# Rope keys of the latent attention spread by transfers within SBUF, and block 2's selection rows written by ScalarE instead of GpSimd

## The chip, the cores and the metric

The kernel runs on one core of one Trainium2 chip. The metric is the device time of one execution in microseconds, as the median of several runs. A core has five engines that each work through their own instructions in order: TensorE (PE; its weight loads are listed apart as PEld), VectorE (DVE), ScalarE (ACT), GpSimd (POOL) and SyncE (SP, which here only issues transfers). ACT and POOL issue transfers too, from the same queue in which their arithmetic stands.

## The reference, cut to what matters

The input is 512 tokens of width 1024. Two layers of a first kind of block are followed by two layers of a second kind.

```
for l in range(2):      # first kind
    c_q, c_kv, k_r, ... = split(x @ w_in)        # latents of MLA; mLSTM; SSD
    q = rmsnorm(c_q) @ w_uq                      # 8 heads x (64 nope + 32 rope)
    k_nope, v = split(rmsnorm(c_kv) @ w_ukv)
    k_rope = rope(k_r)                           # ONE rope key, the same for all 8 heads
    s = (q_nope . k_nope + q_rope . k_rope) * 96 ** -0.5 ;  o = softmax(s) @ v
    x = layernorm(alpha * x + concat(o, mlstm, ssd) @ w_out)
    x = layernorm(alpha * x + moe(x))            # 16 experts in 4 groups, top 2
for l in range(2):      # second kind
    x = x + attention2(rmsnorm(x))               # several kinds of heads, two with differences
    x = x + swiglu(rmsnorm(x))                   # fg, fu, fd
```

The rope key of a token is shared by the eight heads of the latent attention (MLA). All of it is computed in float32, which the kernel reaches by splitting each operand into a high and a low f16 half and adding three matmuls.

## The kernel before, in words

Everything runs on chip memory (SBUF) in tiles of 128 partitions. A token block is 128 tokens, so there are four of them, called t0 to t3. Each projection loads a 128x1024 piece of the weights (`wst`), splits it on ACT (`wh`, L135) and DVE (`wl`, L136), and multiplies with three matmuls (L151 to L153) into PSUM. Normalisations take a reciprocal square root by an integer guess and Newton steps on DVE, a few small instructions that depend on each other (helper lines L159 to L170; the tiles end in `_rs` and `_rsq`). The program is written once, and a scheduler sets the order of the instructions on each engine from it when it is built. An instruction then starts when its engine has come to it and what it reads is there.

`mla()` runs in both layers of the first kind. It makes eight tiles `mlak`: for four heads a high and a low one. The lower 64 partitions get the head's own keys (`mlak<-gK`, L145 on ACT and L146 on DVE), and the upper 64 the shared rope keys `krh`, which POOL copies in once (L674), before any head's own keys are known. A head h uses tile h % 4, so the rope half serves both rounds. The first reader is the matmul `sM` (L703). Beside the start of this function the program still works on the SSD part: `xs` is normalised (L980, after the small steps on `ssd_rs`) and transposed by PE (`mixT`, L298), and POOL copies `mqz` (L1028) for the mLSTM.

`mix2()` runs in both layers of the second kind. It makes two tiles `kl` of 128x4x512 in f16, which carry on half of their partitions a head's low key halves and on the other half selection rows: a constant pattern `selq` that lets the matmul over `kl` (L1864) take the row maxima off the scores. At the start of each layer both tiles are filled with the pattern whole (L1556), and the key half is written later for each group of heads. What stands around it at layer 0: the end of the mixture of experts, whose sums `ysum` (L1438, L1440) go through a layernorm (`ln_...`, `mx`) and the rmsnorm (`xn_...`, `xn`, L236 on ACT, L242 on DVE) into the transposes `xT` (L184) and their eviction `xTh` (L145). At layer 1 the tiles are free earlier than the layer begins, so the scheduler puts the filling into the attention of layer 0 (its softmax: `pe` L761, `pt` L764 and L765, and `o` L800 and L804) and what follows is the projection of layer 0's mixed heads (`px`, loaded from `res` by a transfer that ACT issues, L321).

Of the kernel before, what the change touches and what calls it, by code (L numbers as in the profile page):

```python
# [12 lines left out]
F16 = mybir.dt.float16  # L13
BF16 = mybir.dt.bfloat16
I32 = mybir.dt.int32
AF = mybir.ActivationFunctionType
# [5 lines left out]
P = 128  # L22
T = 512
# [24 lines left out]
class Kern:  # L48
# [377 lines left out]
    def mixer1(self, l, cur):  # L426
# [12 lines left out]
        with self.pool("la") as la:  # L439
# [19 lines left out]
            with r("qm") as qm, r("m1") as m1:  # L459
                with r("s1") as self.q1, r("s2") as s2:  # L460
                    sd = self.ssd_tiles()
                    for b in (2, 4, 0, 3, 5, 1):
                        self.ssd_conv(b, pr, xh, xl, cC, cD, sd, u)
                    self.ssd_gate(xh, xl, cC, sd, u)
                    c0, c1 = (self.ssd_core(s2, m1, g, pr, sd, u) for g in range(2))
                    for c in (c0, c1, c0, c1, c0, c1, c0, c1):
                        next(c, None)
                cE = load("wB", 3, 512)
                cB = load("wB", 0, 512)
                ml = self.mlstm_proj(qm, pr, xh, xl, cE, cB, u)  # L470
                mo = [self.p2.tile([P, NT, P], F32, tag="mo", name="mo", bufs=2) for i in range(2)]
                og = ml[-1]
                with r("ml") as p:
                    self.ptp, self.npt = p, (5, 2)
                    mla = self.mla(p, l, lat)
                    next(mla)
                    for h in range(4):
                        self.mlstm_head(m1, h, mo[h // 2], *ml)
                        if h > 1:
                            (self.mlstm_norm(0, mo[0], og) if h == 2 else self.mix_part(p1, 4, mo[0]))  # L480
                        if h == 3:
                            self.mlstm_norm(1, mo[1], og)
                        next(mla, None)
                    self.mix_part(p1, 5, mo[1])
                    for _ in mla:
                        pass
# [179 lines left out]
    def mla(self, p1, l, lat):  # L666

        nc, p2 = self.nc, self.p2
        cq, ckv, krh = lat

        Kt = [[p1.tile([P, T], F16, name="mlak%d%d" % (h, i)) for i in range(2)] for h in range(4)]
        for h in range(4):
            for i in range(2):
                nc.gpsimd.tensor_copy(Kt[h][i][64:128], krh[i][64:128])  # L674
        wq = [self.wload(self.ap["w_uq"][l], 2048, WS_UQ) + (2,)]
        wkv = [self.wload(self.ap["w_ukv"][l], 1024, WS_UKV) + (1,)]
        v = self.values(p1, "mlav", 8, 64, 0, 8)
        for t in range(NT):
            ps = self.acc("gV")
            self.mm3(ps, ckv[0][:, 0, t * P:(t + 1) * P], ckv[1][:, 0, t * P:(t + 1) * P],  # L680
                     wkv[0][0][:, 512:1024], wkv[0][1][:, 512:1024], True, True)
            self.put_values(v, t, ps, 1.0 / (AS * WS_UKV))
        scale = 96.0 ** -0.5
        HG = 2
        Q, K = {}, {}

        def project(g):

            mx = self.max_tile()
            for i, h in enumerate(range(g * HG, (g + 1) * HG)):  # L690
                Q[h] = [p1.tile([P, T], F16, tag="mq%d" % i, name="mlaq%d" % i, bufs=4) for i in range(2)]
                K[h] = Kt[h % 4]
                ps = self.fm_gemm(cq[0], cq[1], wq, 1024, h * P, P, "gQ")
                tmp = p2.tile([P, T], F32, tag="tmp", name="qtmp", bufs=2)
                nc.vector.tensor_tensor(tmp, ps, self.tab, op=ALU.mult)
                self.split(Q[h][0], Q[h][1], tmp, 1.0 / WS_UQ)
                if h % 2 == 0:
                    kps = self.fm_gemm(ckv[0], ckv[1], wkv, 1024, h * 64, P, "gK")
                self.split(K[h][0][0:64], K[h][1][0:64], kps[64 * (h % 2):64 * (h % 2) + 64],
                           1.0 / WS_UKV)  # L700
                for t in range(NT):
                    ps = self.acc("sM")
                    nc.tensor.matmul(ps, Q[h][0][:, t * P:(t + 1) * P], K[h][0], start=True, stop=True)  # L703
                    nc.vector.tensor_reduce(mx[:, t, i:i + 1], ps, axis=AX.X, op=ALU.max)  # L704
            nc.vector.tensor_scalar(mx[:, :, :HG], mx[:, :, :HG], -1.0 / 256, None, op0=ALU.mult)
            mrow = p2.tile([P, T], F16, tag="mrow", name="mrow")
            nc.scalar.activation(mrow, self.max_rows(mx), AF.Copy)
            return mrow

        mrow = project(0)  # L710
        for g in range(8 // HG):
            yield
            nrow = project(g + 1) if (g + 1) * HG < 8 else None
            for i, h in enumerate(range(g * HG, (g + 1) * HG)):
                pt = self.softmax_T(
                    lambda s, ps, st: [
                        self.mm3(ps, K[h][0][:, s * P:(s + 1) * P], K[h][1][:, s * P:(s + 1) * P],
                                 Q[h][0], Q[h][1], True, False),
                        nc.tensor.matmul(ps, self.sel[:, i, :], mrow, start=False, stop=True)],
                    scale, [0] * NT, v[0] is None)  # L720
                o = self.pso("o")
                for t in range(NT):
                    self.pv(o[:, t * 66:t * 66 + 65], [(pt[s], t, self.value(v, s, h)) for s in range(NT)])
                if h % 2 == 0:
                    mx_ = p1.tile([P, NT, P], F32, tag="mo", name="mo")
                self.norm_out(o, 66, 64, mx_[:, :, 64 * (h % 2):64 * (h % 2) + 64])
                if h % 2:
                    self.mix_part(p1, h // 2, mx_)
            mrow = nrow
# [820 lines left out]
    def mix2(self, l, cur):  # L1550
        nc, b1 = self.nc, self.b1
# [1 line left out]
        u = 1.0 / (AS * WS_IN)  # L1553
        self.kl2, self.turn2 = [b1.tile([P, 4, T], F16, name="kl2%d" % i) for i in range(2)], 0
        for kl in self.kl2:
            nc.gpsimd.tensor_copy(kl, self.selq.unsqueeze(2).to_broadcast([P, 4, T]))  # L1556

        gq = b1.tile([P, 6, 64], F32, name="qkg")
        self.bcast_row(gq.rearrange("p a b -> p (a b)"), self.ap["qk_g"][l], 384)
# [501 lines left out]
```

## Time and profile before

| what | value |
|---|---|
| median of 3 runs (lowest, highest) | 2430.69 us (2425.39, 2432.09) |
| the profiled execution, its own time | 2429.33 us |
| span in its trace | 2427.6 us |
| mean granted clock of TensorE | 0.966 |
| instructions | 34940 |

All rows below come from that one profiled execution. Its span is 1.7 us shorter than its own time, and its own time is 1.4 us below the median of the runs. Times in the rows are counted from the start of the span.

### The profile page before, as it was taken

How to read it: one execution, taken by the hardware profiler on the slowest of the kernel's cores; microseconds unless marked ns; L12 is line 12 of the kernel's file. 1: busy time of each engine (PE TensorE's matmuls, PEld its weight loads, DVE VectorE, ACT ScalarE, POOL GpSimd, SP SyncE). 2: the span in 40 equal slices, each digit the busy share in tenths (PEclk: the TensorE clock that was granted, in tenths of full speed). 3: DMA queues.
4: the chain of work that ended last, by engine and by line, in shares of the span. 5: the costliest groups of instructions: out<-in, count | busy, mean ns of one | idle time of the engine just before them, and what ended most of it. 6: DMA issues, size and time to landing. Idle time of an engine off the chain costs nothing.

```text
span 2427.6 us, 34940 instructions
## 1 busy us (share of the span) xinstructions
PE 2218.0 (91%) x13462; PEld 1215.2 (50%) x13462; DVE 1690.5 (70%) x3602; ACT 1148.7 (47%) x1965; POOL 288.9 (12%) x345
## 2 busy tenths in 40 slices
PE   8888979888889789879998999999998989999999
PEld 4545546544546455434455554444444556544444
DVE  7978887778978977778999654442569996544421
ACT  5546648736547557725544433332345455422220
POOL 2221023231311133211000100000001000000000
PEclk9999989999999989989999999999999989999999
DMA  5311479943312769832212252222332112422222
GB/s 185 119 65 45 174 261 292 313 157 105 115 42 79 276 216 316 295 117 91 87 44 87 77 183 103 94 98 97 118 104 72 51 70 72 164 103 104 104 81 76
DMA packets 61278, 318.80 MB, mean 131 GB/s; under 512 B 12369, under 2 KB 12625, under 8 KB 32688
## 3 DMA queue, kind: packets, MB, share of 16 engines
q1 hardware_dynamic: 41600, 267.87, 31.0%
q0 software_dynamic: 14896, 31.85, 4.9%
q10 hardware_dynamic: 4608, 16.78, 1.8%
q8 instruction: 107, 1.75, 0.3%
q14 instruction: 67, 0.55, 0.1%
HBM read 290.78 MB, written 35.09 MB: 134 GB/s over the span
## 4 chain that ended last, share of the span: by engine, by line
PE 41%; DVE 10%; issue 5%; ACT 5%; DMA 3%; POOL 1%; POOLq 0%; ACTq 0%; DVEq 0%
PE fd L151 3%; PE fd L153 3%; PE fd L152 3%; PE fg L152 3%; PE fu L152 3%; PE fg L153 3%; PE fu L153 3%; PE fg L151 3%; PE fu L151 3%; PE o L800 2%; DMA res<-yt,sidx 2%; DVE wl L136 1%; PE gqk L151 1%; PE gqk L152 1%; PE gqk L153 1%
## 5 line engine op out<-in xcount | busy, mean ns | idle before, releaser
L136 DVE SCALAR_TENSOR_TENSOR wl<-wst,wh 128x1024 f16<-128x1024 f32 (+1 forms) x428 | 514.9, 1231 | 196.8 <-ACT wh L135 195.8
L135 ACT ACTIVATE wh<-wst 128x1024 f16<-128x1024 f32 (+1 forms) x428 | 429.7, 1047 | 270.8 <-PE fd L153 107.2
L152 PEld LDWEIGHTS <-wh 128*128 128x128 f16 x968 | 95.5, 99 | 102.2 <-issue 4.3
L153 PEld LDWEIGHTS <-wl 128*128 128x128 f16 x968 | 95.6, 99 | 101.4 <-issue 2.8
L151 PEld LDWEIGHTS <-wh 128*128 128x128 f16 x968 | 95.9, 99 | 99.8 <-issue 2.1
L152 PE MATMUL fd<-wl,fhh 128*128 128x512 f16 x352 | 133.6, 379 | 0.0
L153 PE MATMUL fd<-wh,fhl 128*128 128x512 f16 x352 | 133.6, 379 | 0.0
L151 PE MATMUL fd<-wh,fhh 128*128 128x512 f16 x352 | 133.6, 379 | 0.0
L151 PE MATMUL gqk<-wh,xTh 128*128 128x512 f16 x320 | 122.9, 384 | 7.6 <-ACT rsq L1736 7.3
L152 PE MATMUL gqk<-wl,xTh 128*128 128x512 f16 x320 | 122.7, 383 | 0.0
L153 PE MATMUL gqk<-wh,xTl 128*128 128x512 f16 x320 | 122.4, 383 | 0.0
L153 PE MATMUL fg<-xTh,wl 128*128 128x512 f16 x320 | 121.4, 379 | 0.0
L151 PE MATMUL fg<-xTh,wh 128*128 128x512 f16 x320 | 121.4, 379 | 0.0
L152 PE MATMUL fg<-xTl,wh 128*128 128x512 f16 x320 | 121.4, 379 | 0.0
L151 PE MATMUL fu<-xTh,wh 128*128 128x512 f16 x320 | 121.4, 379 | 0.0
L152 PE MATMUL fu<-xTl,wh 128*128 128x512 f16 x320 | 121.4, 379 | 0.0
L153 PE MATMUL fu<-xTh,wl 128*128 128x512 f16 x320 | 121.4, 379 | 0.0
L152 PEld LDWEIGHTS <-xTh 128*128 128x128 f16 x768 | 75.0, 99 | 73.9 <-issue 15.6
L151 PEld LDWEIGHTS <-xTh 128*128 128x128 f16 x768 | 74.8, 99 | 67.8 <-ACT xTh L145 5.1
L153 PEld LDWEIGHTS <-xTl 128*128 128x128 f16 x768 | 74.4, 99 | 65.6 <-issue 4.0
L1911 DVE SCALAR_TENSOR_TENSOR fth<-fth,fg 128x512 f32<-128x512 f32 x40 | 27.5, 688 | 107.4 <-ACT fth L1910 107.4
L151 PE MATMUL gO<-wh,mTh 128*128 128x512 f16 x256 | 97.8, 383 | 3.2 <-DVE mx L704 1.7
(613 smaller groups left out, 5489.1 us busy)
## 6 DMA issues: line engine op xcount, KB each, us to landing
wst<-in_w_gu SPq DMA_DIRECT2D x108, 1024.0 KB
wst<-in_w_dn SPq DMA_DIRECT2D x52, 1024.0 KB
wst<-in_w SPq DMA_DIRECT2D x28, 1024.0 KB
wst<-in_wB SPq DMA_DIRECT2D x16, 1024.0 KB
wst<-in_w_out SPq DMA_DIRECT2D x16, 1024.0 KB
dk<-d_nc SPq DMA_DIRECT2D x16, 512.0 KB
res<-xa SPq DMA_DIRECT2D x16, 512.0 KB
rows<-xrow SPq DMA_DIRECT2D x8, 512.0 KB
```

Of the source, the lines that this page charges most:

```text
L135: nc.scalar.activation(wh[:, a:b], st[:, a:b], AF.Copy, scale=scale)
L136: (eng or nc.vector).scalar_tensor_tensor(wl[:, a:b], st[:, a:b], scale, wh[:, a:b], op0=ALU.mult, op1=ALU.subtract)
L151: mm(out, ah, bh, start=start, stop=False)
L152: mm(out, ah, bl, start=False, stop=False)
L153: mm(out, al, bh, start=False, stop=stop)
L800: mm(out, p[:, bs], v, start=first, stop=last)
L1911: nc.vector.scalar_tensor_tensor(th, th, 1.0, pg, op0=ALU.add, op1=ALU.mult)
```

## The change

Two edits. In `mla()` the eight tiles become one, with the four heads' places next to each other, and two transfers within SBUF, issued from POOL's queue, take the place of the eight copies: each reads one half of `krh` (64 partitions x 512 f16) and writes it four times, 256 KB. In `mix2()` the two fillings of `kl` are the same copies, as ScalarE activations of kind Copy.

```diff
     def mla(self, p1, l, lat):
-        Kt = [[p1.tile([P, T], F16, name="mlak%d%d" % (h, i)) for i in range(2)] for h in range(4)]
-        for h in range(4):
-            for i in range(2):
-                nc.gpsimd.tensor_copy(Kt[h][i][64:128], krh[i][64:128])
+        kt = p1.tile([P, 2, 4, T], F16, name="mlak")
+        for i in range(2):
+            nc.gpsimd.dma_start(kt[64:128, i], krh[i][64:128].unsqueeze(1).to_broadcast([64, 4, T]))
+        Kt = [[kt[:, i, h] for i in range(2)] for h in range(4)]
     def mix2(self, l, cur):
         for kl in self.kl2:
-            nc.gpsimd.tensor_copy(kl, self.selq.unsqueeze(2).to_broadcast([P, 4, T]))
+            nc.scalar.activation(kl, self.selq.unsqueeze(2).to_broadcast([P, 4, T]), AF.Copy)
```

On POOL, at the start of the latent attention of layer 0 (`dk` is a decay matrix of the SSD part, `mlavh` the values' low tile), a piece of the difference:

```order
 L872 TENSOR_TENSOR dk<-dk,m_gt 128x512
-L674 COPY mlak_1532<-krh_594 64x512
-L674 COPY mlak_1533<-krh_595 64x512
-L674 COPY mlak_1534<-krh_594 64x512
-L674 COPY mlak_1535<-krh_595 64x512
-L674 COPY mlak_1536<-krh_594 64x512
-L674 COPY mlak_1537<-krh_595 64x512
-L674 COPY mlak_1538<-krh_594 64x512
-L674 COPY mlak_1539<-krh_595 64x512
+L673 DMA mlak<-krh_594 64x4x512
+L673 DMA mlak<-krh_595 64x4x512
 L779 MEMSET mlavh 128x32x2
```

The two transfers stand where the eight copies stood. The order on the other engines is the same there, and so it is in layer 1.

On ACT, at the start of block 2 in layer 0 (`xn` is the rmsnorm of a token block, `vv` and `vvh` the values of a token block out of `gV`), before:

```order
L271 DMA res<-mx 128x1024
L236 ACTIVATE xn,xn_a<-mx 128x512 x2
L786 ACTIVATE vv<-gV_12141 128x4x64
L145 ACTIVATE vvh<-gV_12141 128x4x64
L786 ACTIVATE vv<-gV_12199 128x4x64
L145 ACTIVATE xTh<-xT 128x4x128 x2
L145 ACTIVATE vvh<-gV_12199 128x4x64
L1680 ACTIVATE lps<-lps 128x2
```

and with the change:

```order
L271 DMA res<-mx 128x1024
L236 ACTIVATE xn,xn_a<-mx 128x512 x2
L1556 ACTIVATE kl_11974<-selq 128x2048
L145 ACTIVATE xTh<-xT 128x4x128 x2
L1556 ACTIVATE kl_11975<-selq 128x2048
L786 ACTIVATE vv<-gV_12115 128x4x64
L145 ACTIVATE vvh<-gV_12115 128x4x64
L786 ACTIVATE vv<-gV_12173 128x4x64
L145 ACTIVATE vvh<-gV_12173 128x4x64
L1680 ACTIVATE lps<-lps 128x2
```

The two fillings stand around the evictions `xTh` of the last token block, and the evictions of `gV` of two token blocks come behind both. PE's matmuls of that `gV` move behind some of the `gqk` ones with it.

On ACT, in the projection behind layer 0's attention of block 2, where layer 1's fillings are put (`mTh` is the mixed heads, transposed), before:

```order
L321 DMA px<-res 128x1024
L145 ACTIVATE mTh<-mixT 128x512
L321 DMA px<-res 128x1024
L236 ACTIVATE xn,xn_a<-px 128x512
L271 DMA res<-px 128x1024
L236 ACTIVATE xn,xn_a<-px 128x512
L271 DMA res<-px 128x1024
L236 ACTIVATE xn,xn_a<-px 128x512 x2
L1680 ACTIVATE lps<-lps 128x2
L321 DMA px<-res 128x1024
L145 ACTIVATE xTh<-xT 128x4x128 x2
L321 DMA px<-res 128x1024
```

and with the change:

```order
L321 DMA px<-res 128x1024
L145 ACTIVATE mTh<-mixT 128x512
L321 DMA px<-res 128x1024
L1556 ACTIVATE kl_17815<-selq 128x2048
L271 DMA res<-px 128x1024
L236 ACTIVATE xn,xn_a<-px 128x512 x2
L271 DMA res<-px 128x1024
L236 ACTIVATE xn,xn_a<-px 128x512 x2
L1556 ACTIVATE kl_17816<-selq 128x2048
L145 ACTIVATE xTh<-xT 128x4x128 x2
L321 DMA px<-res 128x1024 x2
```

One filling stands ahead of the first token block's `xn`, the other ahead of its `xTh`, and the load of the third token block's `px` moves behind that `xTh`.

## Rows read from the trace of the kernel before

**Rows 1.** The page's part 1: busy time, share of the span, instructions.

```profile
PE 2218.0 (91%) x13462; PEld 1215.2 (50%) x13462; DVE 1690.5 (70%) x3602; ACT 1148.7 (47%) x1965; POOL 288.9 (12%) x345
```

**Rows 2.** POOL by line: busy us, mean ns; idle before and its releasers.

```profile
L1556 POOL COPY kl<-selq 128x2048 f16<-128x2048 f16 x4 | 7.5, 1888 | 60.2 <-PE sT L1869 31.6 <-PE ysum L1438 15.4 <-PE sT L1866 13.3
```

**Rows 3.** Timeline of POOL, DVE, PE, layer 0: start us, us, engine, operation.

```profile
132.07 5.92 POOL L674 COPY mlak<-krh 64x512 f16<-64x512 f16 x8 [4.46 <-DVE ssd_rsq L168]
...
138.83 0.75 POOL L1028 COPY mqz<-ml 64x512 f32<-64x512 f32 x1
...
132.54 0.57 DVE L169 TENSOR_TENSOR ssd_rsq<-ssd_rsq,ssda 128x4 f32<-128x4 f32 x1
...
135.82 1.70 DVE L136 SCALAR_TENSOR_TENSOR wl<-wst,wh 128x1024 f16<-128x1024 f32 x1
...
137.93 0.16 DVE L977 TENSOR_SCALAR ssda<-ssda 128x4 f32<-128x4 f32 x1
...
139.73 1.21 DVE L136 SCALAR_TENSOR_TENSOR wl<-wst,wh 128x1024 f16<-128x1024 f32 x1
...
142.93 0.16 DVE L169 TENSOR_TENSOR ssd_rsq<-ssd_rsq,ssda 128x4 f32<-128x4 f32 x1
...
143.91 1.14 DVE L980 SCALAR_TENSOR_TENSOR xs<-xs,ssd_rs,sng 128x128 f32<-128x128 f32 x4
...
138.65 0.74 PE L298 MATMUL mixT<-idf,xs 128*128 128x128 f32 x2 [3.19 <-DVE xs L980]
...
145.15 0.27 PE L298 MATMUL mixT<-idf,xs 128*128 128x128 f32 x1
```

**Rows 4.** Windows: length, busy PE, PEld, DVE, ACT, POOL, clock, DMA share, GB/s.

```profile
139.00:140.00 1.00, 1.00 (x5) 0.68 (x5) 1.00 (x4) 0.00 (x0) 0.58 (x1) 0.50 0.00 0
```

**Rows 5.** Waits between 640 and 700 us (layer 1): total, times, longest.

```profile
PE mixT L298 <- DVE xs L980: 3.3, 1, 3.3
```

**Rows 6.** The tiles `mlak` and `q`: their first matmul, and transfers' landing.

```profile
L703 PE MATMUL sM<-mlak,mlaq x64: 376/379/634, 169.2 to 758.2; 128*128 128x512 f16 x64
...
DMA to landing us min/median/max: 2.2/2.3/5.9
```

**Rows 7.** Timeline of POOL, DVE, PE at the start of block 2, layer 0.

```profile
1057.00 3.72 POOL L1556 COPY kl<-selq 128x2048 f16<-128x2048 f16 x2 [15.39 <-PE ysum L1438]
...
1057.19 1.71 DVE L170 SCALAR_TENSOR_TENSOR xn_rs<-xn_rsq,xn_rs 128x1 f32<-128x1 f32 x1
1058.82 1.91 DVE L166 SCALAR_TENSOR_TENSOR ln_rsq<-ln_rs,ln_rsh 128x1 f32<-128x1 f32 x1
...
1063.72 1.94 PE L184 MATMUL xT<-idf,xn 128*128 128x128 f32 x8 [5.50 <-DVE xn L242]
```

**Rows 8.** The chain that ended last, its earliest listed piece and two more: start us, us.

```profile
871.58 1.06 ACT wx L135
...
1058.90 1.84 DVE ln_rsq L166
...
1337.18 1.16 DVE d_rsq L169
```

**Rows 9.** Timeline of DVE in layer 0's attention of block 2.

```profile
1366.56 0.88 DVE L765 TENSOR_TENSOR pt<-pe,pt 128x384 f16<-128x384 f32 x2
...
1370.02 2.60 DVE L765 TENSOR_TENSOR pt<-pe,pt 128x384 f16<-128x384 f32 x2 [0.32 <-ACT pt L764]
```

**Rows 10.** Timeline of ACT, block 2, layer 0, at four places.

```profile
1092.87 0.39 ACT L786 ACTIVATE vv<-gV 128x256 f32<-128x256 f32 x1 [2.77 <-PE gV L153]
...
1172.06 1.91 ACT L1767 ACTIVATE qst<-ra 128x2048 f16<-128x2048 f32 x1
...
1378.28 0.63 ACT L236 ACTIVATE xn<-px 128x512 f32<-128x512 f32 x1 [2.77 <-DVE px L325]
...
1385.62 1.08 ACT L145 ACTIVATE xTh<-xT 128x512 f16<-128x512 f32 x2 [1.76 <-PE xT L184]
```

**Rows 11.** The window of the mixture of experts, layer 0; columns as in rows 4.

```profile
353.00:483.00 130.00, 120.87 (x781) 75.67 (x779) 99.18 (x174) 101.97 (x142) 38.40 (x25) 0.96 0.92 298
```

## The prediction

> **What bounds the kernel now.** The page's first part comes first: PE is busy for 91% of the span, POOL for 12% [rows 1]. POOL is not the bound, and a copy on it costs nothing by itself. So the question is who waits while it copies. What is removed is small: four fillings of 1.89 us [rows 2], and in each layer of the first kind eight copies that take 5.92 together [rows 3], 19.4 us of POOL in all. The timeline of the stretches in which they run shows what stands beside them.
>
> In layer 0's latent attention the eight copies fill 132.07 to 137.99, and DVE's operations beside them stretch. A step on 128x4 elements takes 0.57 us there and 0.16 us at 142.93; a `wl` split takes 1.70 against 1.21 at 139.73 [rows 3]. Both read two operands in SBUF, as do all the stretched DVE instructions below; L977, which reads one, takes 0.16 at 137.93, though that is at the copies' very end. PE then stands still for 3.19 us until DVE has `xs` (L980) for the transposes `mixT` [rows 3], and its granted clock in the stretch behind it is 0.50, which is 1.2 of the 2.4 GHz ([rows 4], one of three such windows, 139 to 142). Layer 1 repeats it with a wait of 3.3 us [rows 5].
>
> In block 2 the two copies at 1057.00 hold two 128x1 steps for 1.71 and 1.91 us, inside a wait of PE of 5.50 us [rows 7]; the chain of work that ended last runs through them (one stands in [rows 8]). In layer 0's attention a third copy holds a `d_rsq` step for 1.16 us, which stands on that chain too [rows 8], and a fourth stretches two `pt` products from 0.88 to 2.60 us [rows 9].
>
> The Trainium skill ("SBUF — State Buffer", section "Who interferes with whom") says that a VectorE instruction with two SBUF inputs and a GpSimd instruction that reads SBUF exclude each other, each for its whole length. The trace agrees: 0.16 becomes 0.57 beside copies of 0.74 (5.92 / 8), and a step of the same kind on 128x1 becomes 1.91 beside copies of 1.89. By that page alone one would remove every such copy; what it gives here hangs on whether PE waits for the DVE instruction, which only the rows say.
>
> **The change part by part.**
>
> *Latent attention, layer 0.* Removed: eight copies. Added: two transfers of 256 KB from POOL's queue. From 132.54 to 137.93 DVE does seven small steps and one `wl` in 5.4 us. Without copies a small step costs 0.2: between 142.93 and 143.91 there are five [rows 3]. Seven of them and a `wl` of 1.21 make 2.6. So `xs` comes 2.8 earlier, and PE's wait of 3.19 falls to 0.4. PE then goes on at 135.85. From there to the second `mixT` it took 6.5 (138.65 to 145.15), 3 us of it at half clock; if the stall of 3 us is what took the clock down, these 3 us lose 1.5, and PE comes to the second `mixT` at 140.85. DVE is there later: the second `xs` moves from 143.91 to 141.1, and its first of four parts is done some 0.3 behind (1.14 / 4), so PE starts at about 141.5 instead of 145.15: 3.65 earlier. Against it stands the copy `mqz`, 0.75 at 138.83 [rows 3], which still reads SBUF and comes earlier, into the same DVE work; at most it takes 0.6 of it back, and I take all of that. **3.0**; the bounds are 2.2 (2.8 - 0.6, the clock falls anyway) and 4.3 (2.8 + 1.5).
>
> The transfers lie beside this work. The nearest row is another transfer within SBUF from the same queue (L1714, as large), which lands 2.3 us after issue, at most 5.9; the first reader of the rope half is `sM` at 169.2 [rows 6]. Issued at 132, they have some 30 us. Without that cover the price would be 2.3 to 5.9 us of PE in each layer. The waits that they add are PE's at `sM`, and with the keys landed at 138 these are no waits.
>
> The same skill page (section "SBUF: two separate sides") warns that descriptors of a transfer issued by GpSimd are written by GpSimd itself and starve while VectorE holds the port; its example is 620 ns alone and about 3100 ns beside a copy. That speaks against this change. The row of L1714 (2.2 to 5.9) may show such a spread, but no row tells what caused it. Five times the median, by that page, would be 11.5 us, still inside the 30, so the sum is the same by either.
>
> *Layer 1* has the same work in the same order: **3.0**, with the same bounds.
>
> *Block 2, start of layer 0.* The two steps of 1.71 and 1.91 need 0.2 each: 3.2 less, and PE's 5.50 has room for it. What stands behind on POOL, the copies for the rotary tables, comes 3.7 us earlier and may hold another step for 0.8 (about one copy of L674): 2.4 at the least, 3.6 if the two cost nothing. On ACT the filling is new. The nearest row is the 2048-element activation at 1172.06: 1.91 us [rows 10]. The first goes into a gap, for ACT waits 2.77 for `gV` at 1092.87 and that eviction now stands behind. The second is behind the last `xTh` and ahead of four `gV` evictions; PE has the `gqk` matmuls of other tokens meanwhile, which moved ahead. I take nothing, and 1.9 as the other end. **3.2** (0.5 to 3.6).
>
> *Layer 1's fillings.* Removed: 1.0 at `d_rsq` (1.16 to 0.16) and 1.7 at `pt` (2.60 to 0.88), 2.7 together; PE waits behind both. Added: two fillings on ACT in the projection. The first lies in front of `xn`, where ACT waits 2.77 for `px`: hidden. The second lies in front of `xTh`, where ACT waits 1.76 for PE [rows 10]: 0.15 sticks out. The load of the third token block's `px` moves from ahead of that `xTh` to behind it, 1.1 to 3.0 later (1.08, with 1.91 or not). I take 0.5 for all of it; if the load is on the path and both fillings are too, it is up to 3.8 (2 x 1.91). **2.2** (-1.1 to 2.7).
>
> **Sum**: 3.0 + 3.0 + 3.2 + 2.2 = 11.4 us. The profiled execution takes 2429.3, its span of 2427.6 and 1.7 around it; it is 1.4 below the median of the runs. That gives **2418** us. The four lower bounds add to 3.8 and the upper ones to 14.9: 2425.5 and 2414.4.
>
> **The rivals.** *The latent attention's gain is given back.* Behind both layers' attention comes the mixture of experts, in whose window the DMA engines are 92% busy at 298 GB/s [rows 11]. If the weights' stream sets the pace there, PE arrives 3 us early and waits 3 us longer. For it: the share of 0.92, and that the chain that ended last can be followed back only to 871.58 [rows 8], so no view shows that the two waits at `mixT` reach the end. Against it: PE is busy for 120.9 of those 130 us, and a load starts when a buffer comes free, which moves with PE. Then 3.2 + 2.2 = 5.4 remains: **2424**.
>
> *ACT takes POOL's place, on the slower side.* ACT works in order and feeds PE (`xTh`, the evictions of `gV`). If each of the four fillings stands in PE's way in full, and the stall takes the clock down to 0.50 for 3 us as at 139, each costs 1.91 + 1.5 = 3.4, and four 13.6 against the gross gain of 11.9 (3.0 + 3.0 + 3.2 + 2.7): 1.7 more than before, **2431**, and up to 2439 where the latent attention's 6 us and the load of `px` go too. It decides at the point where `xTh` waits for the filling and not for PE. Against it: three of the four fillings meet gaps of 1.8 to 2.8.
>
> *The change doesn't do what it says.* Other copies of POOL (the `mqz` copy, the tables of block 2) slide into the freed time and hold the same DVE steps, or those steps were never what `xs` waited for: ACT's squares were. Then a filling's 1.7 in the attention is about all that remains: **2427**. Against it: `mqz` has 0.75 where L674 had 5.92.
>
> **How the numbers follow.** Some 0.3%, 7.3 us, is what a measurement of this kernel can tell from no change. Forecast 0.60, gain given back 0.24, ACT in the way 0.09, nothing done 0.07. Faster by more than that, under 2423.4 on the median: nine tenths of the forecast's 0.60 and a quarter of the second's 0.24, together 0.60. Slower: half of ACT's 0.09, 0.05. The rest, 0.35, is within it. The range: below, the upper bounds give 2414, and the runs of before went down to 5 us under their median, so 2410; above, the second case and most of the last are in with 2429. What is left out is ACT's case and the far tail below.
>
> **What would show it.** In the changed kernel's timeline L674 has no copy on POOL, and L169 beside `xs` is back at 0.16 to 0.2 at all places. PE's wait at `mixT` for `xs` falls from 3.2 to under 1 in both layers, and the windows behind it have a clock of 1.00. The wait of `xT` for `xn` falls from 5.5 to about 2.3. No wait of `sM` names a DMA. The chain has no step of `xn_rs`, `ln_rsq` or `d_rsq` over 0.3. L1556 takes about 1.9 on ACT, and `xTh` still waits for PE. It would be wrong if the mixture's window grows by what the attention lost, if the clock still falls to 0.50 at `mixT`, or if `xTh` or PE's `gV` now waits for L1556.

## The result, and the profile after

The changed kernel takes 2416.03 us (median of 6 runs, 2409.14 to 2422.89) against 2431.39 before (6 runs); the ratio is 0.9937, with an interval of 0.9919 to 0.9955. It is 15.4 us faster. The forecast was 2418 in a range of 2410 to 2429, and the measured time lies inside it. The profiled execution took 2409.14, the fastest of the six, so its span of 2407.4 is 20.2 us shorter than before's, and some 5 us of that are not the change.

The same views of the changed kernel. Part 1 of the page:

```profile
PE 2211.9 (92%) x13458; PEld 1211.8 (50%) x13462; DVE 1677.1 (70%) x3602; ACT 1156.7 (48%) x1969; POOL 273.0 (11%) x329
```

The timeline of POOL, DVE and PE in layer 0's latent attention, to be read against [rows 3]:

```profile
131.06 1.31 POOL L673 DMA_DIRECT2D mlak<-krh  x2 [5.28 <-issue]
...
133.16 0.60 POOL L1028 COPY mqz<-ml 64x512 f32<-64x512 f32 x1
...
131.13 0.16 DVE L169 TENSOR_TENSOR ssd_rsq<-ssd_rsq,ssda 128x4 f32<-128x4 f32 x1
...
133.41 1.44 DVE L136 SCALAR_TENSOR_TENSOR wl<-wst,wh 128x1024 f16<-128x1024 f32 x1 [1.14 <-ACT wh L135]
...
135.56 0.59 PE L298 MATMUL mixT<-idf,xs 128*128 128x128 f32 x2 [0.25 <-DVE xs L980]
...
140.87 0.33 PE L298 MATMUL mixT<-idf,xs 128*128 128x128 f32 x1 [0.19 <-DVE xs L980]
```

The first step L169 is at 0.16 where it was at 0.57, and PE's wait for `xs` fell from 3.19 to 0.25. Of these 2.94, only 1.68 is `xs` coming earlier, counted from the first held step (131.13 to 135.56, where it was 132.54 to 138.65); for the rest PE itself comes later. A new wait stands in the second DVE row: `wl` now waits 1.14 for ACT's half of the split. The stretch behind `mixT` in layer 0, and PE's waits for `xs` in layer 1 ([rows 4, 5] before):

```profile
136.00:137.00 1.00, 1.00 (x9) 0.84 (x8) 1.00 (x4) 1.00 (x2) 0.00 (x0) 1.00 0.00 0
...
PE mixT L298 <- DVE xs L980: 0.8, 2, 0.6
```

The granted clock is 1.00 there now. Just ahead of this place it is the other way round. PE waits 2.57 us for `sti`, a tile of the SSD part, in both profiles; behind that wait the clock was at 1.00 before and is at 0.50 here. Before, with a window behind the wait:

```profile
129.35 0.92 PE L962 MATMUL ssI<-sst,bc 128*128 128x256 f32 x4 [2.57 <-DVE sti L965]
...
130.00:131.00 1.00, 1.00 (x9) 0.66 (x8) 1.00 (x5) 0.99 (x6) 0.00 (x0) 1.00 0.00 0
```

and in the changed kernel, with the `wh` that `wl` then waits for:

```profile
127.52 1.45 PE L962 MATMUL ssI<-sst,bc 128*128 128x256 f32 x4 [2.57 <-DVE sti L965]
...
130.00:131.00 1.00, 1.00 (x6) 0.89 (x5) 1.00 (x3) 0.00 (x0) 0.00 (x0) 0.50 0.08 16
...
132.32 1.06 ACT L135 ACTIVATE wh<-wst 128x1024 f16<-128x1024 f32 x1 [0.29 <-PE gE L152]
```

The rope keys' tile, its first reader and its transfers ([rows 6]):

```profile
L703 PE MATMUL sM<-mlak,mlaq x64: 376/379/634, 165.1 to 747.7; 128*128 128x512 f16 x64
...
DMA to landing us min/median/max: 3.1/3.7/4.0
```

The keys are there by 136.4 (131.06 + 1.31 + 4.0) and read first at 165.1. The start of block 2 ([rows 7]) and the products `pt` of layer 0's attention ([rows 9]):

```profile
1046.76 0.15 DVE L170 SCALAR_TENSOR_TENSOR xn_rs<-xn_rsq,xn_rs 128x1 f32<-128x1 f32 x1
1046.82 0.22 DVE L166 SCALAR_TENSOR_TENSOR ln_rsq<-ln_rs,ln_rsh 128x1 f32<-128x1 f32 x1
...
1048.99 1.06 PE L184 MATMUL xT<-idf,xn 128*128 128x128 f32 x8 [1.19 <-DVE ln_a L197]
...
1353.58 0.56 DVE L765 TENSOR_TENSOR pt<-pe,pt 128x384 f16<-128x384 f32 x1 [0.32 <-ACT pt L764]
1354.30 0.42 DVE L765 TENSOR_TENSOR pt<-pe,pt 128x256 f16<-128x256 f32 x1 [0.16 <-ACT pt L764]
```

PE's wait ahead of `xT` fell from 5.50 to 1.19, and the transposes themselves from 1.94 to 1.06, as the clock behind the stall no longer falls. The two `pt` products that took 2.60 together take 0.98. ACT's timeline at the four fillings ([rows 10]):

```profile
1072.43 1.91 ACT L1556 ACTIVATE kl<-selq 128x2048 f16<-128x2048 f16 x1
1076.46 1.08 ACT L145 ACTIVATE xTh<-xT 128x512 f16<-128x512 f32 x2 [2.12 <-PE xT L184]
1077.43 1.91 ACT L1556 ACTIVATE kl<-selq 128x2048 f16<-128x2048 f16 x1
...
1357.36 1.90 ACT L1556 ACTIVATE kl<-selq 128x2048 f16<-128x2048 f16 x1
...
1364.63 1.89 ACT L1556 ACTIVATE kl<-selq 128x2048 f16<-128x2048 f16 x1
...
1367.37 1.08 ACT L145 ACTIVATE xTh<-xT 128x512 f16<-128x512 f32 x2 [0.84 <-PE xT L184]
```

Behind each of the two fillings that stand in front of `xTh`, ACT still waits for PE, 2.12 and 0.84 us. None of the four is on the chain that ended last.

### The profile page after: what moved, and what is told of

It is laid out like the page before. It is cut to its first block, busy times and chain, and to the rows that moved or that the text cites. A ratio compares the mean times of both kernels' runs of the same rounds, so it can differ in the third digit from the quotient of the medians.

```text
span 2407.4 us, 34925 instructions
## 1 busy us (share of the span) xinstructions
PE 2211.9 (92%) x13458; PEld 1211.8 (50%) x13462; DVE 1677.1 (70%) x3602; ACT 1156.7 (48%) x1969; POOL 273.0 (11%) x329
## 4 chain that ended last, share of the span: by engine, by line
PE 42%; DVE 10%; ACT 5%; issue 4%; DMA 3%; POOL 1%; POOLq 0%; ACTq 0%; DVEq 0%
PE fd L152 3%; PE fd L151 3%; PE fd L153 3%; PE fg L153 3%; PE fu L153 3%; PE fg L151 3%; PE fu L151 3%; PE fu L152 3%; PE fg L152 3%; PE o L800 2%; DMA res<-yt,sidx 1%; DVE wl L136 1%; PE gqk L151 1%; PE gqk L152 1%; PE gqk L153 1%
```

## The experiments

The theory: a GpSimd instruction that reads SBUF holds a VectorE instruction that reads two operands there, and PE waits for the held ones. The rivals: any busy GpSimd does that; block 2 gains by its new order instead; the latent attention's gain is given back in the mixture of experts.

The table shows where each profiled execution gains. For every VectorE instruction its start is compared with that of the same instruction in the kernel before, and the median shift of the nine nearest to a time of before is taken. A column is the change of that shift between two such times, in us; negative is a gain.

```
                     125-  210-  640-  680- 1050- 1067- 1270- 1425-
                      210   640   680  1050  1067  1270  1425  2415
changed kernel       -2.3  -1.6  -4.5  -0.3  -5.0  -1.5  -2.4  -0.9
changed, again (e9)  -2.5  -1.5  -4.3  -0.8  -5.0  -1.9  -4.3  +2.1
transfers only (e1)  -3.9  +0.3  -4.2  +1.7   0.0  -1.4  +0.7  +0.9
the same (e10)       -2.3  -0.1  -4.2  +5.5   0.0  -1.6  +6.3  -1.6
ScalarE only (e2)    +0.6  -1.4  +0.5  +4.1  -5.0  -0.9  -3.9  -2.5
the same (e11)       +0.2  +0.6  -0.5  +2.8  -5.0  -0.8  -3.9  -2.2
writes only (e3)     -2.6  -0.2  -4.4  +4.1  -5.0  -1.6  +0.4  +3.3
short copies (e5)    -2.5  -1.8  -4.5  -0.8  -3.1  -0.1  -1.4  +3.1
half by copies (e6)  -2.0  -0.4  -2.6  -0.3  -5.0  -1.9  -3.5  +1.5
mqz moved (e7)       -2.8  +1.8  -4.6  +4.2  -5.0  +0.7  -3.6  -1.5
ACT's queue (e8)     -3.0  +3.4  -4.2  +1.1  -5.0  -1.9  -3.5  +1.6
```

The first, third, fifth and seventh columns hold the four places of the change. The others show what two executions differ by anyway, up to 5.5 us. All rows are taken against one execution of the kernel before, so what was odd in that one stands in all of them.

**One edit at a time (e1, e10 and e2, e11).**

```diff
 e1, e10: as the changed kernel, but in mix2
+            nc.gpsimd.tensor_copy(kl, self.selq.unsqueeze(2).to_broadcast([P, 4, T]))
-            nc.scalar.activation(kl, self.selq.unsqueeze(2).to_broadcast([P, 4, T]), AF.Copy)
 e2, e11: the kernel before, with the edit in mix2 alone
```

> Only the first edit: the rope keys by two transfers, the fillings of kl stay on GpSimd. If each part does its own work (theory): the first layers' gain is there in full and block 2 is as before, about 5.5 to 6.5 us less than before (2.8 and 3.4 in the two layers), and the steps xn_rs and ln_rsq still take 1.7 and 1.9 beside L1556. If the latent attention's gain is given back in the mixture of experts: less than 2 us, and the mixture's window is longer than in the kernel before by what came in earlier.

> Only the second edit: the fillings on ScalarE, the eight copies stay. Theory: PE still waits 3.2 us for xs in both layers, with the clock at 0.50 behind it; block 2 gains 5 to 6.5 us. If block 2's gain needs the first edit, or came from chance: under 3.

> The first edit alone again, in more rounds, since its first interval ran from 6.3 us less to 1.0 more. By the first profile the two stretches at mixT gained 3.9 and 4.2 us. If that reaches the end: 5 to 9 us less than before. If the mixture of experts gives a part of it back: 0 to 4 us less.

> The second edit alone again, beside the first on the same chip: by its first profile block 2's start gained 5.0 to 5.8 us and layer 1's fillings 3 to 4; 7 to 10 us less than before, and with the first edit's gain the changed kernel's 15.

Transfers only: 2426.23 us against 2431.22, ratio 0.9989 (0.9974 to 1.0004); in the second series 2426.18 against 2430.9, 0.9977 (0.9960 to 0.9993). ScalarE only: 2421.4, 0.9964 (0.9950 to 0.9977), and 2421.28, 0.9962 (0.9947 to 0.9977). In the first, DVE's steps in block 2 are held as in [rows 7]:

```profile
1052.36 1.72 DVE L170 SCALAR_TENSOR_TENSOR xn_rs<-xn_rsq,xn_rs 128x1 f32<-128x1 f32 x1
1054.00 1.91 DVE L166 SCALAR_TENSOR_TENSOR ln_rsq<-ln_rs,ln_rsh 128x1 f32<-128x1 f32 x1
```

In the second, layer 1's wait at `mixT` is there in full, and the window behind layer 0's has the clock of [rows 4]. Layer 0's wait itself was 2.23 in e2 and 3.21 in e11, where 3.2 was expected of both: in e2, as in the changed kernel, the clock was at 0.50 behind the wait for `sti`, and PE came late. The rows of e2:

```profile
PE mixT L298 <- DVE xs L980: 3.3, 1, 3.3
...
140.00:141.00 1.00, 1.00 (x4) 0.61 (x4) 1.00 (x3) 0.00 (x0) 0.46 (x1) 0.50 0.00 0
```

Each edit gains at its own places and nowhere else (the table). The second is worth about 9 us in both series; the first measures 2.7 and 5.6 us by the ratios (5.0 and 4.7 between the medians), while its two columns add to 6.5 to 8.1. e10 was to decide between 5 to 9 us and 0 to 4; its interval, 1.7 to 9.7, does not.

**GpSimd as busy, but only writing (e3).**

```diff
-        Kt = [[kt[:, i, h] for i in range(2)] for h in range(4)]
+        Kt = [[kt[:, i, h] for i in range(2)] for h in range(4)]; scr = p1.tile([P, 320], F16, name="scr"); [nc.gpsimd.memset(scr[64:128], 0.0) for _ in range(16)]
-            nc.scalar.activation(kl, self.selq.unsqueeze(2).to_broadcast([P, 4, T]), AF.Copy)
+            nc.gpsimd.memset(kl, 0.0)
```

> GpSimd is as busy as before in all places but only writes: behind the two transfers stand 16 memsets of a scratch tile, and the fillings of kl are memsets of zero on GpSimd (this leaves the selection rows out). Theory (reading SBUF is what holds VectorE): L169 stays at 0.16, xn_rs and ln_rsq at 0.2, PE's wait at mixT stays under 1 us, and the time is that of the changed kernel or up to 2 us less, since ScalarE is spared 7.6 us. Rival (any busy GpSimd holds VectorE): the steps are at 0.5 and 1.7 to 1.9 again, and the time is that of before. Second rival (block 2 gained by the new order of PE and ScalarE): the steps are short and yet block 2's start is some 2 to 4 us longer than in the changed kernel.

Measured: 2416.55, ratio 0.9943 (0.9923 to 0.9962), the changed kernel's time. Block 2's start in its timeline of POOL, DVE and PE, and two DVE steps of the latent attention with what POOL did beside them:

```profile
1054.26 3.55 POOL L1556 MEMSET kl<- 128x2048 f16 x2 [15.34 <-PE ysum L1438]
...
1054.45 0.14 DVE L170 SCALAR_TENSOR_TENSOR xn_rs<-xn_rsq,xn_rs 128x1 f32<-128x1 f32 x1
1054.51 0.21 DVE L166 SCALAR_TENSOR_TENSOR ln_rsq<-ln_rs,ln_rsh 128x1 f32<-128x1 f32 x1
...
1056.67 1.07 PE L184 MATMUL xT<-idf,xn 128*128 128x128 f32 x8 [1.18 <-DVE ln_a L197]
...
136.33 0.74 POOL L1028 COPY mqz<-ml 64x512 f32<-64x512 f32 x1
137.13 4.94 POOL L674 MEMSET scr<- 64x320 f16 x12
...
136.52 0.57 DVE L169 TENSOR_TENSOR ssd_rsq<-ssd_rsq,ssda 128x4 f32<-128x4 f32 x1
...
139.59 0.16 DVE L169 TENSOR_TENSOR ssd_rsq<-ssd_rsq,ssda 128x4 f32<-128x4 f32 x1
```

The memsets fill the same 3.6 us at the same place as the copies of [rows 7], and the two steps take 0.14 and 0.21. In the latent attention most memsets fell behind the small steps, so that place tests less; but one kernel shows both cases there, the same step at 0.57 beside a copy and at 0.16 beside a memset. A busy GpSimd is not the cause; one that reads SBUF is. The order of ACT and PE is that of before here, and block 2's start still gains 5.0 (fifth column), so the new order is not the cause either.

**The fillings in short copies (e5).**

```diff
-            nc.scalar.activation(kl, self.selq.unsqueeze(2).to_broadcast([P, 4, T]), AF.Copy)
+            [nc.gpsimd.tensor_copy(kl[:, h, c:c + 256], self.selq[:, h:h + 1].to_broadcast([P, 256])) for h in range(4) for c in (0, 256)]
```

> Each filling of kl is eight GpSimd copies of 128x256 instead of one of 128x2048; the transfers stay. Theory (one instruction excludes the other for its whole length, and no longer): the steps xn_rs and ln_rsq take at most 0.2 and one short copy, some 0.45 each, so that about 2.6 of block 2's 3.2 come without ScalarE. Rival (the two share a bandwidth): the steps are slowed as before for as long as GpSimd copies, about 3.6 us together, and block 2 stands as before.

Measured: 2420.97, ratio 0.9960 (0.9940 to 0.9980). POOL, DVE, PE and a window behind `xT`:

```profile
1046.90 7.00 POOL L1556 COPY kl<-selq 128x256 f16<-128x256 f16 x16 [12.53 <-PE ysum L1438]
...
1047.23 0.42 DVE L166 SCALAR_TENSOR_TENSOR ln_rsq<-ln_rs,ln_rsh 128x1 f32<-128x1 f32 x1
1047.58 0.41 DVE L166 SCALAR_TENSOR_TENSOR xn_rsq<-xn_rs,xn_rsh 128x1 f32<-128x1 f32 x1
...
1050.24 1.92 PE L184 MATMUL xT<-idf,xn 128*128 128x128 f32 x8 [2.11 <-DVE xn L242]
...
1052.00:1053.00 1.00, 1.00 (x4) 0.35 (x4) 0.87 (x2) 0.81 (x2) 1.00 (x4) 0.50 0.00 0
```

The held steps take 0.4 instead of 1.9, and PE's wait is 2.11 instead of 5.50. As much data is copied, so what matters is how long one instruction is, as the whole-length exclusion has it; a shared bandwidth would have slowed the steps as before. The gain at this place is 3.1 of 5.0, and the clock still falls to 0.50 behind the wait of 2.11.

**Half of the rope keys by copies (e6).**

```diff
-        for i in range(2):
-            nc.gpsimd.dma_start(kt[64:128, i], krh[i][64:128].unsqueeze(1).to_broadcast([64, 4, T]))
+        nc.gpsimd.dma_start(kt[64:128, 0], krh[0][64:128].unsqueeze(1).to_broadcast([64, 4, T]))
+        [nc.gpsimd.tensor_copy(kt[64:128, 1, h], krh[1][64:128]) for h in range(4)]
```

> Half of the rope keys (the high tiles) by one transfer, the other half by four GpSimd copies; block 2 as in the changed kernel. Theory: VectorE is held for about half as long (four steps at 0.57 instead of 0.16 to 0.2, so some 1.5 us), PE waits for xs about 1 to 2 us instead of 0.25 and 3.19, and what the clock does after a stall of that size is open: at 0.50 the stretch behind mixT loses as in before, at 1.00 it does not. If the stall's length does not depend on the number of copies: 3.2 us again.

Layer 1, PE and the window behind:

```profile
656.75 0.59 PE L298 MATMUL mixT<-idf,xs 128*128 128x128 f32 x2 [1.71 <-DVE xs L980]
...
657.00:658.00 1.00, 0.94 (x6) 0.44 (x5) 1.00 (x4) 0.00 (x0) 0.69 (x2) 1.00 0.00 0
```

In layer 1 the wait follows the number of copies (3.3 with eight [rows 5], 1.71 with four, at most 0.6 with none); in layer 0, where PE came late behind a clock of 0.50, it is 0.64 with four. Behind 1.71 the clock stayed at 1.00. The gain in layer 1 is 2.6 instead of 4.4. One execution took 2415.48.

**mqz by transfers, and the rope keys from ACT's queue (e7, e8).**

```diff
 e7:
-        nc.gpsimd.tensor_copy(qz[r], q[i][r])
+        nc.gpsimd.dma_start(qz[r], q[i][r])
 e8:
-            nc.gpsimd.dma_start(kt[64:128, i], krh[i][64:128].unsqueeze(1).to_broadcast([64, 4, T]))
+            nc.scalar.dma_start(kt[64:128, i], krh[i][64:128].unsqueeze(1).to_broadcast([64, 4, T]))
```

> The changed kernel, and the mLSTM's mqz copies (eight of 0.6 to 0.75 us) as transfers too. Theory: the one wl that took 1.44 beside mqz in layer 0 and the L169 that took 0.57 in layer 1 are back at 1.2 and 0.16; 0.2 to 0.9 us less than the changed kernel in those two places, nothing that the runs can tell. Rival: the transfers come later than the copies did (3 to 4 us instead of 0.6), the mLSTM waits for them, and it is 1 to 5 us slower than the changed kernel.

> The changed kernel, with the two transfers of the rope keys issued from ScalarE's queue. Theory: with 30 us until the first reader it does not matter from where they come: PE's waits at mixT and sM are those of the changed kernel. If descriptors written by GpSimd are held up by VectorE, these transfers land sooner after issue than the 3.1 to 4.0 us from GpSimd's queue.

With `mqz` by transfers (2.2 us to landing) `wl` and L169 are at 1.23 and 0.16 or less in both layers, as expected. The time is 2419.38, ratio 0.9944 (0.9925 to 0.9964), which is not told apart from the changed kernel's in the same series (0.9932, e9). The rival, that the mLSTM waits for the transfers, is not seen: no wait in this trace names one of them. From ACT's queue, the rope keys changed neither PE's wait at `mixT` (0.54 in layer 1) nor any at `sM`; ACT came to issue them at 144.1, 13 us later than POOL, and its trace gives no time to landing, so whether transfers from GpSimd's queue are held up by VectorE stays open. It took 2418.43 in one execution.

**The changed kernel again (e9).**

> The changed kernel once more, beside the others of this call: 10 to 20 us under the kernel before, and a second profile of it, to tell what belongs to the change from what differs between two executions.

2414.49 us against 2431.86, ratio 0.9932 (0.9915 to 0.9950). Its profile repeats the first one's columns, except for the seventh (-4.3 where it had -2.4).

## Why the prediction was right, and where it was off

The mechanism was right, and the forecast 2 us from the median. In part that is luck: the gain was forecast at 11.4 and measured at 15.4. The sum was taken off an execution 1.4 us below the median of its runs, and the runs of the kernel before that stood beside the changed one came out 0.7 higher still, which hides 2 of the 4 us. Sized by place, with the mean of the two profiles of the changed kernel:

*Latent attention, layer 0*: predicted 3.0, measured 2.4. From the first held step to the second `mixT` it is 9.74 us (131.13 to 140.87) where it was 12.61 [rows 3], 2.87 less; but the first `mixT` is only 1.68 earlier (4.43 instead of 6.11), not 2.8. The step that failed in these profiles is that DVE runs its eight instructions without a wait: what is late next is ACT's `wh`, 1.14 us (0.84 in e9). That wait hangs on the clock ahead and not on the change. In both profiles the clock is at 0.50 behind the wait for `sti`, and the `wh` follows PE's slow `gE`. In e1 the clock held at 1.00 there, as it had before, and `wl` does not wait:

```profile
130.61 0.92 PE L962 MATMUL ssI<-sst,bc 128*128 128x256 f32 x4 [2.63 <-DVE sti L965]
...
133.80 0.15 DVE L169 TENSOR_TENSOR ssd_rsq<-ssd_rsq,ssda 128x4 f32<-128x4 f32 x1
...
134.89 1.23 DVE L136 SCALAR_TENSOR_TENSOR wl<-wst,wh 128x1024 f16<-128x1024 f32 x1
...
137.24 0.59 PE L298 MATMUL mixT<-idf,xs 128*128 128x128 f32 x2 [0.52 <-DVE xs L980]
...
142.55 0.33 PE L298 MATMUL mixT<-idf,xs 128*128 128x128 f32 x1 [0.18 <-DVE xs L980]
```

(e10, the same kernel with the clock at 0.50 there, waits 1.00.) In e1 the first `mixT` is 2.67 earlier and the second 3.86, against 2.8 and 3.65 in the working, and the place gains 3.9. So like against like the sum holds, and the 2.4 sets a slow stretch against a fast one. That `mqz` takes 0.6 back was too much; it cost `wl` 0.2 in the first profile and one L169 0.4 in e9.

*Layer 1*: predicted 3.0 as in layer 0, measured 4.4, just over the upper bound of 4.3. There `wl` does not wait for `wh`, as in e1's layer 0, which gained 3.9. "The same work in the same order" was taken to mean the same gain; what stands ahead differs, and ACT is ahead here. One sign named in the prediction did not come: an L169 still takes 0.57 here, beside `mqz`.

*Start of block 2*: predicted 3.2, measured 5.0 in every kernel without copies there, over the bound of 3.6. Two things were left out of the sum, both in rows that the prediction had: a wait of 5.50 that goes takes the fall of the clock behind it away too (`xT` 1.94 to 1.06), which was counted at `mixT` and not here. And the tables' copies do not slide into the freed time: in the changed kernel POOL has done them by 1034.4, long before these steps, for they had only stood behind a filling that waited 15.39 us for PE's `ysum` [rows 7]. Before, one of them held a third step for 1.07 us.

*Layer 1's fillings*: predicted 2.2 after a cost of 0.5, measured 3.4 (2.4 and 4.3; ScalarE alone 3.9 both times). Read in shorter pieces in the same way, the part with the two held steps, 1330 to 1378, gains 2.6 and 2.7, just the 2.7 predicted before the cost, and e3 with its memsets gains 3.4 there. What the first profile has less, it lost before 1330, ahead of both steps. The cost is not there: from 1378 to 1425 the seven profiles with the fillings on ScalarE gain another 0.8 to 1.3 us, and those with the fillings on GpSimd lose 0.6 to 6.0, e3 too, so this piece is not the held steps. In the five profiles with the fillings on GpSimd the chain that ended last waits 5.5 to 8.0 us for a weight load of the feed-forward part; in none of the other seven does it. Before, and in e3:

```profile
1402.72 5.48 DMA wst<-in_w_gu
...
1389.75 7.96 DMA wst<-in_w_gu
```

Whether the later load of `px` makes room for it was not tried.

The four together are 15.2, the time 15.4; the other columns add 4.3 and 2.1 us of gain in the two profiles, so the closeness says little. Terms that were 0.6 too large and 1.4, 1.8 and 1.2 too small make 3.8 more than the 11.4 forecast.

*Gain given back in the mixture of experts*, the first rival: the two columns of these stretches go from -1.8 to +3.4 and from -0.8 to +5.5 with the first edit, and without it -1.4, +0.6 and +4.1, +2.8. So nothing is given back that the profiles can show. It is not fully settled: the first edit alone measured 2.7 and 5.6 us where its places gain about 7; the first interval ends at 6.3, the second at 9.7. Against ScalarE alone (0.9962 to 0.9964) the changed kernel (0.9932 to 0.9937) is 0.25 to 0.32% lower, 6 to 8 us, which would be the whole gain; but these are different series, and each interval reaches 3 to 4 us to either side.

*ACT takes POOL's place*: it did not; `xTh` waited for PE behind both fillings. *The change doesn't do what it says*: ACT's squares were not what `xs` waited for, but ACT's `wh` is close behind, as 1.14 shows.

## What to carry to other kernels

Where small VectorE steps on two operands in SBUF stand on the path, look at what GpSimd reads in that moment: a long copy costs a step its own length, and what goes away with it is the stall and, at these places, the slow clock behind it. Such a copy can go to a transfer, where there is slack for its landing (30 us here), to an engine with gaps, or, for part of the gain, into shorter instructions; a memset beside such steps need not be moved. Before pricing a removed wait, ask at each place apart what is late next, and count the clock at every stall, not only at the first. Before sizing a place from two profiles, see whether the clock ahead of it was the same in both.

The same holding was left in ahead of the latent attention. There POOL works on `dk` from two tiles, and a DVE step takes 1.62 beside it, 0.55 behind it, in the kernel before:

```profile
124.49 1.58 POOL L872 TENSOR_TENSOR dk<-dk,m_lt 128x512 f32<-128x512 f32 x1
...
124.87 1.62 DVE L1023 TENSOR_TENSOR mqs<-mqs,ml 128x384 f32<-128x384 f32 x1
...
127.95 0.55 DVE L1023 TENSOR_TENSOR mqs<-mqs,ml 128x384 f32<-128x384 f32 x1
```

Three steps in a row are held so, and PE's wait of 2.57 for `sti` comes behind them on DVE. What it would give to move `dk` was not tried.

## What the runs showed of the hardware

The Trainium skill ("SBUF — State Buffer", section "Who interferes with whom") says that a VectorE instruction with two SBUF inputs does not contend with a GpSimd instruction that only writes SBUF; the runs agree, with 0.14 and 0.21 us for the steps beside 3.55 us of memsets. A held step waits for about one instruction of GpSimd: 0.57 beside copies of 0.74, 0.42 beside copies of 0.40, 1.91 beside copies of 1.89. GpSimd waits too: in e5 one of the sixteen short copies took 1.39 where most took 0.40. Short copies also cost by themselves: eight of them took 3.01 us in block 2's attention of layer 0, where one long one took 1.89.

The granted clock was at 0.50 behind stalls of PE of 2.11 (e5), 3.19 and 5.50 us, and at 1.00 behind 1.71 (e6) and 1.19. The length of the stall alone does not settle it: behind the wait for `sti`, 2.57 to 2.69 us in all twelve profiles, the clock was at 0.50 in nine and stayed at 1.00 in three (before, e1, e11), and one kernel profiled twice showed both (e1 and e10, e2 and e11). The low stretch costs beyond its stall: the transposes `xT` took 1.94 us in it and 1.06 out of it.
